# Attention scores and transposes in 64-row tiles of the TensorE array, values as plain fp32 products in two column halves

## The chip, the cores and the metric

The kernel runs on one core of a Trainium2 chip. The metric is the device time of one execution in microseconds (us), lower is better. The engines of the core work side by side: TensorE multiplies matrices (PE in the profile, with its weight loads as PEld), VectorE (DVE), ScalarE (ACT) and GpSimd (POOL) do the rest, and SyncE (SP) issues DMAs. A product of TensorE has a stationary operand, loaded into the array by a weight load, and a moving operand, which streams through column by column; the result lands in PSUM, in banks of 512 fp32 columns.

## The reference

Two layers of multi-head latent attention beside a convolution branch, followed by a gated feed-forward network, over 1024 tokens of width 1024, all in fp32. The change touches the attention alone:

```
q_nope, k_nope: 8 heads x 64      q_rope: 8 heads x 32      k_rope: 32, shared by the heads
sc = einsum("bqhd,bkhd->bhqk", qn, k_nope) + einsum("bqhr,bkr->bhqk", qr, k_rope)
p  = softmax(sc * scale)
o  = einsum("bhqk,bkhd->bqhd", p, v)          # v: 8 heads x 64
```

## The kernel before

Everything fp32 is multiplied as a pair: `hi` is the value rounded to fp32r, the type that TensorE takes at full rate, and `lo` the rest. A product is three products: hi·hi, hi·lo and lo·hi. Activations lie transposed, with channels on the partitions and the 1024 tokens along the row.

A layer has three stages: projections (`project`), attention (`attention`), and output projection with feed-forward network (`feed`). Instructions are emitted in the order of the Python code, and each engine runs its own in that order.

`attention` runs over 64 steps a layer: 8 heads times 8 blocks of 128 queries. In step n, TensorE is given three pieces of work:

- `values` (L1537): the product of exponentials and values. `v` holds for each key block and pair of heads 128 columns: 64 with the high part and 64 with the low part of the values of one head. The exponentials come as `pt`, transposed and split into hi and lo. A step does a quarter of 512 queries: 4 products of 128 rows by 512 columns (L1552) into the bank `o`. After four steps `o` holds the two partial sums in its two halves of the partitions, which ACT and DVE add (L1557, L1558).
- `turn` (L1514): transposes of the exponentials of a pair of query blocks, half of the keys at a time: 8 transposes of 128 by 128 (L1529) into two banks `t`. ACT rounds each bank to `pt` hi (L1531), DVE subtracts to `pt` lo (L1532).
- `scores` (L1492): the scores of the block two steps ahead. The stationary operand is `q` (96 rows: 64 of the head and 32 rotary), the moving one `k`; three products for each half of the keys make 6 of 512 columns (L1500). DVE then takes the maximum (L1502).

`expo` (L1505) is ACT's exponential of the block of the next step. PSUM holds two score tiles of two banks each and four single banks that `t`, `o` and small tiles share.

Beside this a table of 64 steps (`agenda`) places work of other kinds: taps of the long convolution that remain from the projections (`tap_late`, L1703), each of kind "pool" (GpSimd multiplies, a DMA adds), "act" (ScalarE multiplies in two halves, a DMA adds) or "both" (GpSimd multiplies and adds), the division by the sums, the splitting of finished heads, and the loads of the output weights `wo`. `LATE_KINDS` gives the kinds in turn, and `LATE_COST` how far apart they are placed.

Head 0 is put together by DMAs straight from the projections, the others are loaded from DRAM eight steps ahead (`load_head`, L1459).

## Time and profile before

| | us |
|---|---|
| median of 3 runs | 2284.3 (2283.11 to 2286.27) |
| span of the profiled execution | 2282.9 |
| attention of layer 0, about | 200 to 415 |
| attention of layer 1, about | 1330 to 1545 |

The profiled execution is one of the same program. Its span runs from the first to the last instruction; the median of the runs is 1.4 us above it. The granted TensorE clock is 0.999 of full over the span.

How to read it: a busy share says how long an engine had something in work, and an engine that is busy all the time is the bound wherever nothing releases it late. Durations of matmuls overlap, since one starts while the one before is still leaving the array; what a product costs in a row of products is the distance between starts, which the chain of waits gives, and not its own duration.

### The profile page before, as it was taken

How to read it: one execution, taken by the hardware profiler on the slowest of the kernel's cores; microseconds unless marked ns; L12 is line 12 of the kernel's file. 1: busy time of each engine (PE TensorE's matmuls, PEld its weight loads, DVE VectorE, ACT ScalarE, POOL GpSimd, SP SyncE). 2: the span in 40 equal slices, each digit the busy share in tenths (PEclk: the TensorE clock that was granted, in tenths of full speed). 3: DMA queues.
4: the chain of work that ended last, by engine and by line, in shares of the span. 5: the costliest groups of instructions: out<-in, count | busy, mean ns of one | idle time of the engine just before them, and what ended most of it. 6: DMA issues, size and time to landing. Idle time of an engine off the chain costs nothing.

```text
span 2282.9 us, 30530 instructions
## 1 busy us (share of the span) xinstructions
PE 2269.7 (99%) x10684; PEld 1887.8 (83%) x10684; DVE 1730.2 (76%) x2329; ACT 1286.7 (56%) x2043; POOL 781.8 (34%) x810
## 2 busy tenths in 40 slices
PE   9999999999999999999999999999999999999998
PEld 7888888888888888888888888888888888888887
DVE  6989888768877776776559788886697777768665
ACT  5445877646655555544533468774475555555444
POOL 1222787522333333001412237873323333320032
PEclk9999999999999999999999999999999999999999
DMA  6889998946899998935968999967659999989356
GB/s 185 165 175 271 194 200 166 235 138 145 211 277 296 275 296 208 334 106 143 209 136 166 218 255 197 184 149 207 175 129 228 271 302 279 294 210 315 102 124 167
DMA packets 198569, 475.73 MB, mean 208 GB/s; under 512 B 27296, under 2 KB 34576, under 8 KB 198416
## 3 DMA queue, kind: packets, MB, share of 16 engines
q0 software_dynamic: 103136, 222.46, 48.5%
q1 hardware_dynamic: 94992, 250.93, 32.9%
q8 instruction: 84, 1.38, 0.3%
q14 instruction: 69, 0.57, 0.1%
q10 hardware_dynamic: 288, 0.39, 0.0%
HBM read 309.28 MB, written 80.40 MB: 171 GB/s over the span
## 4 chain that ended last, share of the span: by engine, by line
PE 92%; DVE 3%; DMA 1%; POOL 1%; ACT 1%; issue 1%; SPq 0%; DVEq 0%; ACTq 0%; POOLq 0%
PE p L1063 36%; PE pd L1251 18%; PE s L1500 7%; PE po L874 7%; PE o L1552 4%; PE t L1529 4%; PE pa L215 2%; PE pg L215 2%; PE pg L513 2%; DVE conv L1694 2%; PE pq L215 1%; PE pn L215 1%; PE pv L1481 1%; PE pkv L215 1%; PE pa L513 1%
## 5 line engine op out<-in xcount | busy, mean ns | idle before, releaser
L1063 PE MATMUL p<-b,w 128*128 128x512 f32 x3552 | 806.3, 389 | 0.1
L1063 PEld LDWEIGHTS p<-b,w 128*128 128x128 f32 x3552 | 666.4, 188 | 139.3 <-DVE w L1441 0.5
L1251 PE MATMUL pd<-ab,wd 128*128 128x512 f32 (+1 forms) x1920 | 422.3, 381 | 0.0
L1251 PEld LDWEIGHTS pd<-ab,wd 128*128 128x128 f32 x1920 | 350.7, 188 | 69.5 <-DVE ab L1441 0.4
L1500 PE MATMUL s<-k,q 96*128 96x512 f32 x768 | 208.0, 406 | 0.0
L179 POOL DMA_DIRECT2D w<-wu x96 | 84.7, 883 | 360.0 <-ACT w L178 319.1
L1532 DVE TENSOR_TENSOR pt<-t,pt 128x512 fp32r<-128x512 f32 x256 | 164.8, 685 | 53.6 <-ACT pt L1531 51.7
L1711 POOL TENSOR_TENSOR late<-gate,par 128x1018 f32<-128x1018 f32 (+12 forms) x79 | 171.7, 2174 | 18.7 <-issue 9.7
L1531 ACT CAST pt<-t 128x512 fp32r<-128x512 f32 x256 | 137.6, 589 | 65.2 <-PE t L1529 63.6
L1453 DVE SCALAR_TENSOR_TENSOR o<-zg,par,o 128x1023 f32<-128x1023 f32 x88 | 112.7, 1283 | 75.6 <-ACT o L1447 74.3
L179 POOL DMA_DIRECT2D w<-in_w_up x116 | 100.5, 866 | 199.4 <-ACT w L178 175.4
L1502 DVE TENSOR_REDUCE mx<-s 128x1 f32<-128x1024 f32 x128 | 155.8, 1217 | 0.0
L1500 PEld LDWEIGHTS s<-k,q 96*128 96x128 f32 x768 | 135.1, 189 | 22.9 <-ACT p L1510 0.2
L1510 ACT ACTIVATE p<-s,mx 128x1024 f32<-128x1024 f32 x128 | 144.8, 1131 | 1.9 <-DVE mx L1502 1.9
L1694 DVE SCALAR_TENSOR_TENSOR conv<-gate,par,conv 128x1009 f32<-128x1009 f32 (+7 forms) x112 | 142.3, 1274 | 3.6 <-ACT conv L575 1.0
L1552 PE MATMUL o<-pt,v 128*128 128x512 f32 x512 | 140.3, 397 | 0.0
L837 POOL DMA_DIRECT2D wd<-in_w_down x44 | 32.6, 744 | 307.9 <-PE pd L1251 306.9
L1439 ACT CAST ab<-ac 128x512 fp32r<-128x512 f32 x130 | 80.1, 617 | 98.3 <-DVE ac L1186 95.6
L178 ACT ACTIVATE w<-w 128x512 fp32r<-128x512 f32 x212 | 133.6, 630 | 3.0
L1529 PEld LDWEIGHTS t<-ident,p 128*128 128x128 f32 x1024 | 119.6, 140 | 18.5 <-ACT p L1510 1.2
L1529 PE MATMUL t<-ident,p 128*128 128x128 f32 x1024 | 133.3, 273 | 0.7 <-ACT p L1510 0.7
L1012 DVE TENSOR_TENSOR zg<-p,zg 128x512 f32<-128x512 f32 x88 | 60.5, 690 | 96.5 <-PE p L1063 89.6
(2122 smaller groups left out, 4113.9 us busy)
## 6 DMA issues: line engine op xcount, KB each, us to landing
w<-in_w_up POOLq DMA_DIRECT2D x232, 256.0 KB, 7.2
wu<-in_w_up SPq DMA_DIRECT2D x88, 512.0 KB, 6.0
w<-wu POOLq DMA_DIRECT2D x96, 256.0 KB, 5.9
sd<-in_w_down SPq DMA_DIRECT2D x44, 512.0 KB, 10.1
ws<-sd SPq DMA_DIRECT2D x44, 512.0 KB, 7.4
wd<-in_w_down POOLq DMA_DIRECT2D x88, 256.0 KB, 5.3
act<-v SPq DMA_DIRECT2D x36, 512.0 KB, 5.7
ac<-act SPq DMA_DIRECT2D x72, 256.0 KB, 6.1
```

Source lines behind the costliest of these rows:

```text
L179: self.nc.gpsimd.dma_start(out=lo, in_=src, accum_op=ALU.add)
L215: nc.tensor.matmul(ps[:, HALVES[c]], w, x[:, HALVES[c]], start=(k == 0 and s == 0), stop=(k == n - 1 and s == 2))
L874: self.nc.tensor.matmul(ps, p[:, sl], q[:, cs], start=(k == 0 and t == 0), stop=(k == 3 and t == 2))
L1063: nc.tensor.matmul(ps, w[p][:, k * 128:(k + 1) * 128], b[:, q], start=(i in (1, 5, 2) and k == 0 and t == 0), stop=(k == 3 and t == 2), sk ...
L1251: nc.tensor.matmul(ps[t, m][:, cs], w[i, j][p][:, m * 128:(m + 1) * 128], b[:, q, cs], start=(i in (1, 5, 2) and j == 0 and s == 0), stop= ...
L1500: nc.tensor.matmul(ps[:, cs], q[i][0:96, qs], k[j][0:96, cs], start=(s == 0), stop=(s == 2))
L1502: nc.vector.tensor_reduce(out=mx, in_=ps, op=ALU.max, axis=AX.X, negate=True)
L1529: nc.tensor.transpose(tp[:, i, qi * 128:(qi + 1) * 128], st["p"][2 * qp + qi][:, kt * 128:(kt + 1) * 128], self.ident)
L1532: nc.vector.tensor_tensor(out=lo, in0=tp, in1=hi.bitcast(F32), op=ALU.subtract)
L1552: nc.tensor.matmul(po, v[2 * c + i][:, h // 2, e, :], pt[s][:, i, :], start=(c == 0 and i == 0 and s == 0), stop=(c == 3 and i == 1 and s ...
L1694: self.nc.vector.scalar_tensor_tensor(out=y[:, lo:hi], in0=u[:, lo + s:hi + s], scalar=self.tap(l, j, t), in1=y[:, lo:hi], op0=ALU.mult, o ...
L1711: self.nc.gpsimd.tensor_tensor(out=p[:, lo:hi], in0=u[:, lo + s:hi + s], in1=self.tap(l, j, t).broadcast_to([128, hi - lo]), op=ALU.mult)
```

## The change

- **Scores** (`scores`): the array is used as two tiles of 64 rows. Rows 0 to 63 compute the first half of the keys and rows 64 to 127 the second half, each into its own bank. The queries lie twice on the partitions (`qh`, `ql`: 64 rows of the head each; `qr`: 32 rotary rows high and 32 low), and the keys lie with their first half on the upper 64 partitions and the second on the lower (`kn`, and `keys` for the shared rotary part). Five passes of two products take the place of three passes of two.
- **Transposes** (`turn`): 16 transposes of 64 rows by 128 columns, in the same two row tiles, take the place of 8 of 128 by 128. The two tiles write two banks, `t0` and `t1`, of one buffer each. ACT copies `t0` and DVE copies `t1` into `pt`, unsplit, in fp32.
- **Values** (`values`): `v` and `pt` are plain fp32. The products run once for two turns: 8 products of 256 columns for a pair of query blocks. Each has 64 columns of values, and they go by turns to the left and the right column half of the array, with outputs in the two halves of the partitions of `o`. The sum of the halves (`gather`) is put behind the step's other work.
- **PSUM**: two score tiles as before, two shared banks where there were four, and `t0` and `t1`.
- **Heads**: loading a head takes 16 DMAs where it took 10, and the shared rotary keys are laid out once a layer by 8 DMAs.
- **Late taps**: one "act" in five of the first half becomes "pool"; GpSimd's multiplication is a tensor_scalar in place of a tensor_tensor with a broadcast operand; the costs that space the taps are smaller for "pool" and "both".

```diff
-LATE_KINDS = (("pool", "both", "act", "pool", "act"), ("pool", "both", "pool", "pool", "pool"))
-LATE_COST = {"act": 1.1, "pool": 3.5, "both": 4.8}
+LATE_KINDS = (("pool", "both", "act", "pool", "pool"), ("pool", "both", "pool", "pool", "pool"))
+LATE_COST = {"act": 1.1, "pool": 2.4, "both": 3.7}
+ROW_TILES = (slice(0, 64), slice(64, 128))
...
-        with self.psum(f"attn{l}", 2, 4):
+        with self.psum(f"attn{l}", 2, 2):
...
-            vt = self.blk(f"v{l}_{tt}", F32R, (128, 4, 2, 128))
...
+            if tt % 2 == 0:
+                v.append(self.blk(f"v{l}_{tt}", F32, (128, 2, 512)))
+            (nc.vector.tensor_copy if tt % 2 else nc.scalar.copy)(out=v[tt // 2][:, tt % 2], in_=ps)
...
-            for s, (i, j) in enumerate(((0, 0), (0, 1), (1, 0))):
-                for cs in HALVES:
-                    nc.tensor.matmul(ps[:, cs], q[i][0:96, qs], k[j][0:96, cs], start=(s == 0), stop=(s == 2))
+            passes = ((qh, kn, 0), (qh, kn, 1), (ql, kn, 0), (qr, keys, 0), (qr, keys, 1))
+            for s, (w, k, i) in enumerate(passes):
+                for r, cs in zip(ROW_TILES, HALVES):
+                    nc.tensor.matmul(ps[:, cs], w[r, qs], k[r, i, :], start=s == 0, stop=s == len(passes) - 1)
...
-                        nc.tensor.transpose(tp[:, i, qi * 128:(qi + 1) * 128], st["p"][2 * qp + qi][:, kt * 128:(kt + 1) * 128], self.ident)
-                hi, lo = (t[:, :, qs] for t in st["pt"][c, qp // 2])
-                nc.scalar.copy(out=hi, in_=tp)
-                nc.vector.tensor_tensor(out=lo, in0=tp, in1=hi.bitcast(F32), op=ALU.subtract)
+            tp = [self.pp.tile([128, 4, 2, 64], F32, name=f"t{l}_{h}_{qp}{g}{r}", tag=f"t{r}", bufs=1) for r in range(2)]
+            for i in range(4):
+                ks = slice((4 * g + i) * 128, (4 * g + i + 1) * 128)
                 for qi in range(2):
+                    for t, r in zip(tp, ROW_TILES):
+                        nc.tensor.transpose(t[:, i, qi, :], st["p"][2 * qp + qi][r, ks], self.ident[r, r])
+            pt = st["pt"][qp, g] = self.tmp("ws", f"pt{l}_{h}_{qp}{g}", F32, (128, 4, 2, 2, 64))
+            nc.scalar.copy(out=pt[:, :, :, 0, :], in_=tp[0])
+            nc.vector.tensor_copy(out=pt[:, :, :, 1, :], in_=tp[1])
...
-            for s in range(2):
-                for i in range(2):
-                    nc.tensor.matmul(po, v[2 * c + i][:, h // 2, e, :], pt[s][:, i, :],
-                                     start=(c == 0 and i == 0 and s == 0), stop=(c == 3 and i == 1 and s == 1))
+            for g in range(2):
+                pt = st["pt"].pop((qp, g)).rearrange("p k q r t -> p k (q r t)")
+                for i in range(4):
+                    k = 4 * g + i
+                    nc.tensor.matmul(po[ROW_TILES[i % 2], cs], v[k // 2][:, k % 2, h * 64:h * 64 + 64], pt[:, i, :],
+                                     start=k < 2, stop=k > 5)
...
+        for n in range(-2, total + 1):
+            if n % 2 and n > 2:
+                values((n - 3) // 2, n)
+            if n % 2 and n > 0 and n + 1 < total:
+                expo(n + 1)
+            if n > 0:
+                turn(n)
...
-            self.nc.gpsimd.tensor_tensor(out=p[:, lo:hi], in0=u[:, lo + s:hi + s],
-                                         in1=self.tap(l, j, t).broadcast_to([128, hi - lo]), op=ALU.mult)
+            self.nc.gpsimd.tensor_scalar(out=p[:, lo:hi], in0=u[:, lo + s:hi + s], scalar1=self.tap(l, j, t), scalar2=1.0,
+                                         op0=ALU.mult, op1=ALU.mult)
```

TensorE's rows in the middle of head 2 of layer 0, before: one step, with the scores of block 5, a quarter of the values of queries 0 to 511 and half of the transposes of blocks 2 and 3 (`s`, `o` and `t` are the PSUM tiles; `xN` joins equal neighbours).

```order
L1500 MATMUL s_2_5_2396<-k_20_1985,q_20_1983 128x512 x2
L1500 MATMUL s_2_5_2396<-k_21_1986,q_20_1983 128x512 x2
L1500 MATMUL s_2_5_2396<-k_20_1985,q_21_1984 128x512 x2
L1552 MATMUL o_2_0_2414<-pt_2_000_2307,v_0_1579 128x512
L1552 MATMUL o_2_0_2414<-pt_2_000_2307,v_1_1591 128x512
L1552 MATMUL o_2_0_2414<-pt_2_010_2308,v_0_1579 128x512
L1552 MATMUL o_2_0_2414<-pt_2_010_2308,v_1_1591 128x512
L1529 MATMUL t_2_12_2419<-ident,p_2_2_2334 128x128 x2
L1529 MATMUL t_2_12_2419<-ident,p_2_3_2372 128x128 x2
L1529 MATMUL t_2_13_2426<-ident,p_2_2_2334 128x128 x2
L1529 MATMUL t_2_13_2426<-ident,p_2_3_2372 128x128 x2
```

The same place on TensorE after the change: the scores of block 6, then all values of blocks 2 and 3, then the first four of 16 transposes of blocks 4 and 5.

```order
L1500 MATMUL s_2_6_2624<-kn_2_2057,qh_2_2054 128x512 x4
L1500 MATMUL s_2_6_2624<-kn_2_2057,ql_2_2055 128x512 x2
L1500 MATMUL s_2_6_2624<-kr_1132,qr_2_2056 128x512 x4
L1549 MATMUL o_2_0_2553<-pt_2_10_2582,v_0_1590 64x256 x2
L1549 MATMUL o_2_0_2553<-pt_2_10_2582,v_2_1607 64x256 x2
L1549 MATMUL o_2_0_2553<-pt_2_11_2621,v_4_1653 64x256 x2
L1549 MATMUL o_2_0_2553<-pt_2_11_2621,v_6_1705 64x256 x2
L1523 MATMUL t_2_200_2652<-ident,p_2_4_2562 128x64
L1523 MATMUL t_2_201_2653<-ident,p_2_4_2562 128x64
L1523 MATMUL t_2_200_2652<-ident,p_2_5_2637 128x64
L1523 MATMUL t_2_201_2653<-ident,p_2_5_2637 128x64
```

The values now stand in every second step alone, between scores and transposes; the step between has transposes and scores only.

VectorE at that place, before: two subtractions for each turn, and the maximum of a block of scores.

```order
L1532 TENSOR_TENSOR pt_2_010_2308<-t_2_10_2382,pt_2_000_2307 128x2x256
L1532 TENSOR_TENSOR pt_2_011_2310<-t_2_11_2389,pt_2_001_2309 128x2x256
L1502 TENSOR_REDUCE mx_2_5_2403<-s_2_5_2396 128x1
L1532 TENSOR_TENSOR pt_2_012_2346<-t_2_12_2419,pt_2_002_2345 128x2x256
L1532 TENSOR_TENSOR pt_2_013_2348<-t_2_13_2426,pt_2_003_2347 128x2x256
```

VectorE there after the change, with the sum of the halves of `o` (`yt`) between a maximum and the copy behind it, which happens in every second pair of steps.

```order
L1526 COPY pt_2_20_2670<-t_2_201_2653 128x8x64
L1502 TENSOR_REDUCE mx_2_7_2684<-s_2_7_2673 128x1
L1563 TENSOR_TENSOR yt_2_2551<-o_2_0_2553,yt_2_2551 64x512
L1526 COPY pt_2_21_2709<-t_2_211_2692 128x8x64
L1502 TENSOR_REDUCE mx_3_0_2724<-s_3_0_2713 128x1
```

Two subtractions became one copy, which no longer follows a copy of ScalarE; `pt_2_21` is what the second half of the next values reads.

More of the change, by code (lines that the diff above doesn't have):

```diff
@@ L525, in project @@
         kd = [self.dp.tile([HEADS, NOPE, T], F32R, name=f"kd{l}{i}") for i in range(2)]
-        krd = [self.dp.tile([ROPE, T], F32R, name=f"krd{l}{i}") for i in range(2)]
         st = {}
@@ L818, in project @@
         work(1e9)
-        return u, conv, away, (qd, qrd, kd, krd), (kvs, w["v"]), heads
+        return u, conv, away, (qd, qrd, kd), st["keys"], (kvs, w["v"]), heads
     def layer(self, l, carry):
@@ L1535, in turn, with values @@
                     st["p"].pop(2 * qp + qi)
-        def values(group, c, n):
-            h, gg = divmod(group, 2)
+        def values(pair, n):
+            h, qp = divmod(pair, 4)
             st = state[h]
             e = h % 2
+            gg = qp // 2
             main, aux = slice(e * 64, e * 64 + 64), slice(64 - e * 64, 128 - e * 64)
-            if c == 0:
+            if qp % 2 == 0:
                 if gg == 0 and e == 0:
```

93 lines of the change are left out of this document (36 added, 57 removed).

## The prediction

> **What bounds the kernel now.** I read the page from its top: the share of each engine, then the slices of TensorE, then the costliest groups.
>
> ```profile
> PE 2269.7 (99%) x10684; PEld 1887.8 (83%) x10684; DVE 1730.2 (76%) x2329; ACT 1286.7 (56%) x2043; POOL 781.8 (34%) x810
> PE   9999999999999999999999999999999999999998
> ...
> L1500 PE MATMUL s<-k,q 96*128 96x512 f32 x768 | 208.0, 406 | 0.0
> ...
> L1532 DVE TENSOR_TENSOR pt<-t,pt 128x512 fp32r<-128x512 f32 x256 | 164.8, 685 | 53.6 <-ACT pt L1531 51.7
> L1711 POOL TENSOR_TENSOR late<-gate,par 128x1018 f32<-128x1018 f32 (+12 forms) x79 | 171.7, 2174 | 18.7 <-issue 9.7
> L1531 ACT CAST pt<-t 128x512 fp32r<-128x512 f32 x256 | 137.6, 589 | 65.2 <-PE t L1529 63.6
> ...
> L1502 DVE TENSOR_REDUCE mx<-s 128x1 f32<-128x1024 f32 x128 | 155.8, 1217 | 0.0
> ...
> L1510 ACT ACTIVATE p<-s,mx 128x1024 f32<-128x1024 f32 x128 | 144.8, 1131 | 1.9 <-DVE mx L1502 1.9
> ...
> L1552 PE MATMUL o<-pt,v 128*128 128x512 f32 x512 | 140.3, 397 | 0.0
> ```
>
> TensorE is idle for 13 us in all (2282.9 less 2269.7). So the time changes by what TensorE's own work in the attention changes, and by waits that it does not have today. The stage itself, in the view of busy time by windows (the middle of the attention of layer 0; the columns are PE, PEld, DVE, ACT, POOL):
>
> ```profile
> 222.00:390.00 168.00, 168.00 (x953) 142.12 (x952) 140.90 (x177) 134.91 (x244) 136.54 (x89) 1.00 0.89 189
> ```
>
> Nothing but TensorE is full here, at full clock. What a step costs it stands in the chain of waits of that stretch, in order of time (start, length, what):
>
> ```profile
> 222.05 0.93 PE o L1552 x4
> 222.98 0.87 PE t L1529 x8
> 223.85 1.39 PE s L1500 x6
> 225.24 0.94 PE o L1552 x4
> 226.17 0.88 PE t L1529 x8
> 227.05 1.39 PE s L1500 x6
> ```
>
> A step is 3.20 us: values 0.93, transposes 0.87, scores 1.39. One product of 512 columns costs 0.232 (1.39 / 6), one transpose 0.109. Two steps, the unit of the changed kernel, are 6.40 us, and there are 32 such pairs in each of two layers, 64 in all.
>
> **The change, part by part.** I count one pair of steps.
>
> *Scores.* Six products become ten, in five pairs that use different rows of the array and different banks. No two products of the trace use different rows, so the price is bounded: from five times one product (pairs at once) to ten. I take pairs at once, because each product uses only half of the rows, and because the weight loads allow it:
>
> ```profile
> L1500 PEld LDWEIGHTS s<-k,q x768: 186/188/192, 203.2 to 1537.0; 96*128 96x128 f32 x192
> L1500 PE MATMUL s<-k,q x768: 387/393/479, 203.5 to 1537.2; 96*128 96x512 f32 x192
> L1569 PEld LDWEIGHTS sr<-ident,sums x14: 84/84/84, 250.4 to 1521.1; 128*8 128x8 f32 x14
> L1529 PEld LDWEIGHTS t<-ident,p x1024: 137/140/143, 213.0 to 1546.0; 128*128 128x128 f32 x171
> ```
>
> A load of 8 columns takes 84 ns, so some 80 are fixed, and one of 128 columns in the scores (188) occupies about 0.11. Even if ten loads follow each other, they take 1.1 us, beside 5 x 0.232 = 1.16. Two steps: 2.32 in place of 2.78.
>
> *Transposes.* Eight of 128 columns become 16 of 64 columns in row pairs. The moving part of one halves, to 0.055, but each still loads 128 columns of weights: 140 less 84 for 120 columns is 0.060 a load. Pairs that load at once give 8 x 0.060 = 0.48 a turn; loads that follow each other give 16 x 0.060 = 0.96, against 0.87 now. I take pairs at once, for the same reason as in the scores, plus 0.05 at the start of each scores burst, whose loads (0.11) are longer than a transpose that would cover them. Two turns: 1.06 in place of 1.75, with 2.02 as the other end. That choice carries most of the forecast. The Trainium skill speaks for it: TensorE: Matmul & The Clock Gate, Part 3, The mechanism, says that a weight load overlaps matmuls in flight when it goes to another row group. No run here shows it; by that rule the sum stays as it is, and without it the first rival below holds.
>
> *Values.* Eight plain fp32 products of 256 columns replace eight of 512. Plain products stand only at the very start, where eleven of them warm the array; the rows are of the view by line, and of TensorE's timeline:
>
> ```profile
> L397 PEld LDWEIGHTS warm<-ones x22: 289/333/333, 1.1 to 5.5; 128*128 128x128 f32 x22
> ...
> 1.06 5.06 PE L397 MATMUL warm<-ones 128*128 128x128 f32 x22 [1.06 <-DVE ones L372]
> 5.77 0.77 PE L468 MATMUL pg<-xs_0h,wg00h 128*128 128x512 f32 x1
> 7.30 0.50 PE L468 MATMUL pg<-xs_0h,wg00h 128*128 128x512 f32 x1 [0.76 <-ACT xs_0h L415]
> ```
>
> Eleven products are 22 records: a plain product is two loads and two passes. Less the last record's 421 ns, the starts of 22 passes of 128 columns lie over 4.64 us, 0.22 apart. But the load takes 333 ns there against 188 later, and the first full product 0.77 against 0.50, so the array ran at about half speed, whatever clock the profile gives for those microseconds. At full speed 128 columns are 0.11, and a pass of 256 columns 0.22 (the other end, if it was at full speed, is 0.44). Eight products are 16 passes. Each waits for the pass before it in its own column half, and the two passes of one product share a half, so a second pass runs beside the first pass of the next product: nine rounds of 0.22, 1.98 us, in place of 1.87. If the halves do not overlap it is 16 x 0.22 = 3.52; if the first and last pass overlap too, 1.76.
>
> *Changes of form.* In each pair of steps the array goes from row halves to column halves and back. A product's record is 393 ns, its share in a row of products 232: 0.16 us pass until its results are out. I take that once for each change, 0.32. The ends are nothing, and 0.16 plus a whole load, 0.35 each or 0.70. The Trainium skill, TensorEngine Tiling (Array Packing), Key Properties, says that a change of tiling mode drains the array; that speaks against this change, and by it the 0.32 is owed and not the zero. No row of this trace shows a drain.
>
> *Sum.* 2.32 + 1.06 + 1.98 + 0.32 = 5.68, against 6.40.
>
> *What waits instead.* ACT loses two copies of 0.59 in each step for one, DVE two subtractions of 0.69 for one copy that I price at 0.69 as well (a plain copy from PSUM by DVE is not in the trace; 0.59, as on ACT, to 0.69). Per pair DVE has two maxima (1.22), two copies and half a sum of halves (0.69): 4.2 us of 5.68. ACT has two exponentials with their read-out, two copies and half a copy of `o`:
>
> ```profile
> 337.80 0.21 ACT L1510 ACTIVATION_READ_ACCUMULATOR p<-s,mx 128x1 f32 x1
> ```
>
> that is 2 x (1.13 + 0.21 + 0.59) + 0.29 = 4.15. Both fit. But `t0` and `t1` have one buffer each: the second turn waits until both copies of the first are done, 0.16 + 0.69 after its transposes, while the scores between them run for 1.16. So 0.3 us of slack, which a late tap on ACT (0.73) or a cast of a finished head takes away now and then. The values read the second turn's `t1` copy, which stands behind a maximum and every second time behind the sum of halves: 0.2 (tail and signal) + 1.22 + 0.69 + 0.69 = 2.8 us after the scores of that maximum. By then TensorE has the second turn, the next scores and the first half of the values, which reads the first turn's copy: 0.53 + 1.16 + 1.0 = 2.7. That about covers. I add 0.10 a pair for these: **5.78 us, 0.62 less, 40 us in 64 pairs**; the ends of this item are 0 and 0.3.
>
> *The rest.* GpSimd has five more taps a layer; at the old 2.17 us plus 0.93 for their DMA issue that is 15 us of the 31 that it has free in the 168 us window, so costless as long as the stage shortens by less than the other 16. Its new multiplication is not in the trace; at the old price nothing is gained, and a cheaper one only adds slack. The view of waits has the place where it would show:
>
> ```profile
> PE po L874 <- DMA wo<-in_w_o: 1.9, 2, 1.0
> ```
>
> The output weights come by GpSimd's DMAs, behind its last additions, and TensorE already waits for them. With the six more DMAs for each head, which SP issues eight steps ahead, and the shorter cover at both ends I add 5 us (0 to 10). The row of copies for `v` shrinks, off the path.
>
> So 2282.9 - 40 + 5 = 2248, and the median of the runs lies 1.4 above that span: **2249 us**.
>
> **Rivals.**
> - *Weight loads follow each other* although the products do not (slower than before). Place: the 2048 small transposes. Then a turn is 0.96, the pair 6.74, 22 us more than now, with the 5 at the ends **2311**. It decides from 0.54 us more a pair, which is when a transpose costs over 0.047 on average. For it: no row shows two loads at once. Against: no load in the trace goes to other rows than the one before it, so none could show it.
> - *The gain is eaten*: the changes of form cost 0.70 and the copies 0.3 or a little more: 5.68 + 0.38 + 0.3 = 6.36 and the 5 us, **about 2287**, between 2268 and 2300. For it: single buffers, and slack of 0.3 us.
> - *Column halves follow each other*: 3.52 for the values, pair 7.32, **2348**. Against: different columns, different output partitions.
> - *The tiles do not work at once at all*, so the change does not do what it says: 4.64 + 2.02 + 3.52 + 0.42 = 10.6 a pair, **2558**.
> - *Plain passes cost 0.44*: nine rounds 3.96, **2376**.
> - *All hides*: no price for the form, eight rounds: 5.14 a pair and no waits, **about 2204**.
>
> **How the numbers follow.** The forecast (2232 to 2268) has 0.47, the eaten gain 0.17, loads in a row 0.15, all hidden 0.08, column halves in a row 0.07, no overlap 0.03, dear passes 0.03. A measurement tells a difference of about 0.2%, 4.6 us. Faster: 0.47 + 0.08 + 0.06 of the eaten gain = 0.61; within: 0.06; slower: the remaining 0.05 and the other four, 0.33. The range from 2222 to 2318 leaves out part of the hidden case, the column halves, no overlap and dear passes, about 0.2.
>
> **What would show it.** In the changed profile's chain, scores of ten products over 1.16 us a step and 16 transposes over half a microsecond show that rows work at once; 0.96 or more is the first rival, and starts of two loads of a pair 0.06 apart would name it. The values should be 16 records over 2 us, by twos. Gaps ahead of `o` and behind it, without a releaser, are the changes of form; waits of `t` for ACT or DVE the single buffers. TensorE should stay above 97% busy; if it falls, the second rival holds. I am wrong from the root if the ten products of a step take 2.3 us, or if the time of the attention, some 215 us a layer now, does not shrink by about 20.

## The result, and the profile after

| | before | after |
|---|---|---|
| median of the runs, us | 2283.8 (4 runs, 2283.11 to 2286.27) | 2319.6 (4 runs, 2314.6 to 2323.93) |
| ratio, 95% interval | 1 | 1.0154 (1.0136 to 1.0171) |
| span of the profiled execution, us | 2282.9 | 2312.6 |
| first scores to last values, two layers, us | 217.5 + 218.0 | 226.0 + 229.7 |

The change costs 36 us where 35 us of gain were forecast. The profiled execution is the fastest of the four (2314.6 us), so some 5 of the 36 us are not in the trace read here. The page of the changed kernel begins like that of before, and says little:

```profile
PE 2247.6 (97%) x12732; PEld 1798.7 (78%) x12732; DVE 1659.3 (72%) x2177; ACT 1215.3 (53%) x1873; POOL 736.1 (32%) x819
```

TensorE is busy for 22 us less and idles 65 us in place of 13. Now the chain of waits of the changed kernel in the middle of the attention (start, length, what):

```profile
243.97 0.64 PE t L1523 x16
244.61 1.22 PE s L1500 x10
245.83 0.58 PE t L1523 x16
246.41 1.22 PE s L1500 x10
247.62 1.88 PE o L1549 x16
249.50 0.64 PE t L1523 x16
```

Two turns, two scores and the values of a pair: 0.64 + 1.22 + 0.58 + 1.22 + 1.88 = 5.54 us, where the forecast's own work was 5.68 and the kernel before needs 6.40. TensorE does what was expected of it. Pairs that wait for no load start 5.44 to 6.04 us apart, about 5.7 in the mean. The time is lost elsewhere, and the busy time by windows says where. First the kernel before, over the attention of each layer (columns: length, then PE, PEld, DVE, ACT, POOL, granted clock, share of the 16 DMA engines, GB/s), and then the changed one:

```profile
203.50:421.00 217.50, 217.14 (x1217) 183.19 (x1216) 183.25 (x238) 171.65 (x313) 163.91 (x111) 1.00 0.90 205
1333.00:1551.00 218.00, 217.64 (x1219) 183.75 (x1218) 180.83 (x237) 170.71 (x312) 160.25 (x108) 1.00 0.88 200
```

```profile
207.00:433.00 226.00, 204.28 (x2240) 139.42 (x2239) 145.38 (x162) 136.34 (x230) 138.65 (x113) 0.95 0.97 222
1349.80:1579.50 229.70, 201.40 (x2241) 137.46 (x2240) 145.82 (x162) 136.17 (x230) 132.60 (x109) 0.93 0.93 213
...
222.00:390.00 168.00, 156.35 (x1820) 107.37 (x1820) 111.80 (x126) 109.11 (x187) 110.82 (x91) 0.97 1.02 219
```

Three columns matter. TensorE's busy time falls from 434.8 to 405.7, but the windows are 455.7 long: it now idles 50 us, from 0.7. The granted clock falls from 1.00 to 0.95 and 0.93. The stretches at half clock in the two windows last 54.6 us; TensorE is busy for 37.0 of them, and full clock would have saved half of that, some 18 us. And the DMA engines, at 0.89 of the same 168 us before, stand at 1.02. (The share adds up the times of all packets, packets overlap, and it is no hard limit: e6_taps_undone reaches 1.05. That the engines hold the loads up is for the experiments to show.) So the attention's bill is 48 us of work saved (434.8 - 405.7 + 18.5), 18 lost to the clock and 49 to waits, together 20 more; the other 9.5 us of the 29.7 between the spans lie outside these windows. What TensorE waits for, in the view of waits of the changed kernel (total, times, longest):

```profile
PE s L1500 <- DMA kn<-kd: 27.5, 7, 9.3
PE t L1523 <- ACT pt L1525: 11.3, 2, 7.9
PE s L1500 <- DMA ql<-qn: 4.8, 2, 4.1
PE o L1549 <- DVE yt L1563: 4.8, 8, 1.7
```

The first row is the keys of a head, loaded from DRAM, and the third the queries of head 0. The second is ScalarE's copy, held up behind its rounding of output weights that GpSimd's DMAs bring late (8.64 us before 1554.64). The DMA queues over the attention of layer 0, before and after (q0 is GpSimd's, with the additions of the late taps; q1 is SP's, with the loads):

```profile
q0 software_dynamic: 7488, 23.93, 57.3%
q1 hardware_dynamic: 6897, 20.53, 32.3%
```

```profile
q0 software_dynamic: 7474, 23.88, 54.5%
q1 hardware_dynamic: 9864, 25.88, 42.2%
```

GpSimd's queue takes the same 123 to 125 us of 16 engines (57.3% of 217.5, 54.5% of 226). SP's went from 70 to 95 us. Together 195 became 218 us of engine time, and TensorE's own work there, 204 less 11 for the clock, is 193. That makes the transfers the first suspect: the loads, which share the engines with the additions, are what comes late. The 218 are no fixed bill: from 222 to 390 us SP's packets took 160 ns each here (43.1% of 16 engines for 7248 packets), and 187 in e1_no_late_dma (51.1% for 7348), where the additions are left out. SP's queue shows the slow loads (start, length of the issue):

```profile
294.81 3.35 SPq L124 DMA_DIRECT2D qr<-qrd  x2
298.21 0.45 SPq L124 DMA_DIRECT2D kn<-kd  x1
298.70 0.60 SPq L124 DMA_DIRECT2D qh<-qd  x1
299.35 1.93 SPq L124 DMA_DIRECT2D qr<-qrd  x2
301.33 1.54 SPq L124 DMA_DIRECT2D kn<-kd  x1
```

Many issues of a load take 1 to 1.7 us here; in e1_no_late_dma, at a share of 0.54, most take 0.45 to 0.6. (The kernel before has slow ones too, 1.2 to 1.7 us from 282.77 to 287.38, at 0.89.) A load's sixteen last 19 us (from 316.11 to 335.27) of the 22 that a head has at 5.44 us a pair.

A wait costs more than its length. TensorE's timeline at one of them, and the granted clock around it:

```profile
310.58 0.71 PE L1500 MATMUL s<-kn,qh 64*128 64x512 f32 x3
315.31 0.79 PE L1500 MATMUL s<-kn,qh 64*128 64x512 f32 x1 [4.02 <-DMA kn<-kd]
315.31 1.21 PE L1500 MATMUL s<-kn,ql 64*128 64x512 f32 x2
315.90 1.47 PE L1500 MATMUL s<-kr,qr 64*128 64x512 f32 x4
317.31 2.58 PE L1549 MATMUL o<-pt,v 128*64 128x256 f32 x16
...
321.11 0.64 PE L1500 MATMUL s<-kr,qr 64*128 64x512 f32 x4
```

```profile
315.30:318.70 3.40, 3.39 (x15) 1.99 (x17) 1.23 (x1) 0.00 (x0) 2.81 (x4) 0.51 1.04 201
318.70:322.00 3.30, 3.30 (x52) 2.43 (x50) 0.90 (x2) 1.79 (x3) 3.00 (x4) 1.00 1.06 243
```

After an idle gap of 4.0 us TensorE runs at half clock for 3.4 us: four rotary products take 1.47 us in place of 0.64. Half of 3.4 us, 1.7, is lost on top of the 4.0.

### The profile page after: what moved, and what is told of

The parts are those of the page before. It is cut to its first block, busy times and chain, and to the rows that moved or that the text cites. A ratio compares the mean times of both kernels' runs of the same rounds, so it can differ in the third digit from the quotient of the medians.

```text
span 2312.6 us, 34368 instructions
## 1 busy us (share of the span) xinstructions
PE 2247.6 (97%) x12732; PEld 1798.7 (78%) x12732; DVE 1659.3 (72%) x2177; ACT 1215.3 (53%) x1873; POOL 736.1 (32%) x819
## 4 chain that ended last, share of the span: by engine, by line
PE 78%; DMA 10%; DVE 5%; POOL 2%; issue 2%; ACT 2%; SPq 1%; DVEq 0%; POOLq 0%; ACTq 0%
PE p L1066 33%; PE pd L1254 18%; PE po L877 6%; PE s L1500 3%; DMA kn<-kd 2%; PE pa L216 2%; PE o L1549 2%; PE pg L216 2%; DMA conv<-late 2%; PE pg L514 2%; DVE conv L1691 2%; PE pn L216 1%; PE pq L216 1%; DMA wo<-in_w_o 1%; PE t L1523 1%
## 5 line engine op out<-in xcount | busy, mean ns | idle before, releaser
L1526 DVE COPY pt<-t 128x512 f32<-128x512 f32 x128 | 87.9, 686 | 76.0 <-PE t L1523 74.7
L1549 PE MATMUL o<-pt,v 128*64 128x256 f32 x1024 | 133.8, 403 | 6.1 <-DVE yt L1563 4.8
L1708 POOL TENSOR_SCALAR late<-gate,par 128x1018 f32<-128x1018 f32 (+13 forms) x88 | 121.7, 1383 | 12.1 <-PE pn L216 6.3
L1500 PE MATMUL s<-kn,qh 64*128 64x512 f32 x512 | 97.9, 444 | 27.6 <-DMA kn<-kd 27.5
L1456 DVE SCALAR_TENSOR_TENSOR v<-zv,par,v 128x1023 f32<-128x1023 f32 x88 | 112.2, 1277 | 10.5 <-ACT v L1450 10.4
L1549 PEld LDWEIGHTS o<-pt,v 128*64 128x64 f32 x1024 | 70.9, 143 | 61.3 <-issue 26.1
L1442 ACT CAST w<-wu 128x512 fp32r<-128x512 f32 x84 | 51.8, 619 | 122.4 <-DVE wu L1015 122.4
L1523 PEld LDWEIGHTS t<-ident,p 64*128 64x128 f32 x2048 | 78.0, 139 | 49.0 <-issue 26.9
## 6 DMA issues: line engine op xcount, KB each, us to landing
sd<-in_w_down SPq DMA_DIRECT2D x44, 512.0 KB, 10.1
```

Source lines behind the costliest of these rows:

```text
L1456: self.nc.vector.scalar_tensor_tensor(out=o[:, a:b], in0=z[:, at + a:at + b], scalar=self.par[l][:, tap:tap + 1], in1=o[:, a:b], op0=ALU.m ...
L1500: nc.tensor.matmul(ps[:, cs], w[r, qs], k[r, i, :], start=s == 0, stop=s == len(passes) - 1)
L1549: nc.tensor.matmul(po[ROW_TILES[i % 2], cs], v[k // 2][:, k % 2, h * 64:h * 64 + 64], pt[:, i, :], start=k < 2, stop=k > 5)
```

## The experiments

Each ran beside the kernel before on the same chip; its median there is 2283.8 to 2284.7 us. "Pair" is the distance between the starts of two bursts of values.

**The additions of the late taps by DMA, left out** (the convolution's result lacks these taps).

```diff
         if kind == "both":
             ...
-        else:
-            self.nc.gpsimd.dma_start(out=y[:, lo:hi], in_=p[:, lo:hi], accum_op=ALU.add)
```

> The changed kernel without the DMAs that add the late taps of kinds pool and act to the convolution (39 a layer, so those taps are missing from the sum; everything else is the same). Theory DMA: the 16 DMA engines are full in the attention (busy share 0.97 in 203 to 425 us, where the kernel before had 0.89), and these additions are about half of their work, so the head loads land late. Then the waits of the scores for kn and ql (32 us) fall below 6 us, pairs of steps stand at 5.4 to 5.9 us throughout, and the time falls to 2225 to 2250 us. Theory SP: the 16 issues a head and the round trip of the sums in the SyncE queue set when the loads start, whatever the DMA engines do. Then at least half of the waits for kn stay (over 14 us), and the time stays above 2275.

2272.9 us, ratio 0.995 (0.9933 to 0.9967). The waits for keys, and the middle of the attention:

```profile
PE s L1500 <- DMA kn<-kd: 6.2, 4, 2.3
```

```profile
222.00:390.00 168.00, 163.14 (x1945) 111.97 (x1942) 120.00 (x135) 116.60 (x199) 73.31 (x55) 0.98 0.54 111
```

Without them the DMA share falls to 0.54, the loads come nearly in time and 47 us are back: the transfers' part is shown. But the kernel stays above the 2225 to 2250 expected; two slow pairs at the start and two at the end of each layer (10.3 and 7.5, 12.8 and 10.0 us in layer 0; 10.1 and 7.2, 6.8 and 8.3 in layer 1) are still there. So transfers in the middle were not all.

**Half of each load issued by ScalarE**, the second row tile's eight DMAs.

```diff
-                self.move(tiles[p][r, :], qd[p][h])
+                queue = self.nc.scalar if c else None
+                self.move(tiles[p][r, :], qd[p][h], queue)
...
```

> The changed kernel with half of each head's loads (the 8 DMAs of the lower 64 partitions) issued by ScalarE in place of SyncE. The bytes are the same. Theory SP: with 8 issues a head SyncE is done in time, the waits for kn fall from 27 to below 8 us, and the time falls to 2270 to 2290. Theory DMA: the loads share the same full engines, the waits of TensorE for loads stay above 20 us in sum (for whichever tile is last), and the time stays at 2305 to 2340, more if ScalarE is held up by its own issues.

2390.1 us, ratio 1.0464 (1.0449 to 1.048). The waits for keys are gone, and TensorE waits 99.8 us for exponentials instead, 14 times up to 14.3: ScalarE's exponentials stand behind its own issues and what those wait for (63.0 us for key loads alone). Issuing from a second engine only stopped that engine. Since TensorE now comes later to every load, the run decides nothing for SP's queue itself.

**Half of the late additions by GpSimd instead of DMA.**

```diff
-LATE_KINDS = (("pool", "both", "act", "pool", "pool"), ("pool", "both", "pool", "pool", "pool"))
+LATE_KINDS = (("both", "pool", "act", "both", "pool"), ("both", "pool", "both", "pool", "both"))
```

> The changed kernel with about 15 late taps a layer moved from kind pool (a DMA adds) to kind both (GpSimd adds). All taps are computed. About 15 x 3 us of DMA work a layer is gone, 216 to about 171 us, and GpSimd has some 22 us more. Theory DMA: most of the waits for kn go (below 10 us), the time falls to 2235 to 2275. Theory SP: the time stays within 10 us of the changed kernel's 2320, since SyncE's issues are untouched.

2287.9 us, ratio 1.0016 (1.0003 to 1.0028), with the whole computation done: 32 us of the loss are back, less than the DMA theory's 2235 to 2275, far more than the 10 us of the other. What is left of the waits for keys (18.3 us in 4) is all at the load of head 1, which stands on SP's queue behind the spills (the stores to DRAM) of the queries.

**The row tiles one after the other**: in scores and transposes all instructions of one tile, then all of the other; in the values two products of one column half, then two of the other.

```diff
-            for s, (w, k, i) in enumerate(passes):
-                for r, cs in zip(ROW_TILES, HALVES):
+            for r, cs in zip(ROW_TILES, HALVES):
+                for s, (w, k, i) in enumerate(passes):
...
```

> The changed kernel with the same products and transposes in another order: in each group all of one tile first, then all of the other (scores 5 + 5, transposes 8 + 8, values column half 0 twice, then half 1 twice). If it is the alternation that lets two tiles work at once, scores go from 1.22 to about 2.1 us a step, transposes from 0.62 to about 0.9 to 1.0, values from 1.9 to about 3.1 a pair, and the whole to 2450 to 2520 us. If the price is set by something else (loads, or the products' own rate), the durations stay within 10% of the changed kernel.

One time, 2316.0 us: as the changed kernel, where 2450 to 2520 were expected if alternation mattered. The chain of waits (pieces of one or two instructions between these are left out):

```profile
244.00 0.76 PE t L1523 x13
...
244.94 1.08 PE s L1500 x8
...
246.15 0.47 PE t L1523 x10
...
246.80 1.38 PE s L1500 x9
248.19 1.93 PE o L1549 x16
```

A pair takes 6.1 us, 0.65 more than in turns, and not the double: transposes and scores alternate in the chain in pieces smaller than a turn, so one tile's work can still run beside the other's, and the values cost 1.93 with their halves by twos. And 0.65 us x 62 pairs, 40 us more work, cost nothing in this one run: the waits for keys fell from 27.5 to 11.8 us. That fits a stage that is bound by something else.

**A head's load in 8 DMAs in place of 16**, same bytes.

```diff
...
-                for i in range(2):
-                    at = c * 64 + p * ROPE + i * HALF
-                    self.move(tiles[2][at:at + HALF, :], qrd[p][i, h])
-                self.move(tiles[3][r, p, :], kd[p][h][:, HALVES[c]])
+            self.move(tiles[2][r, :], qrd[:, :, h])
+            self.move(tiles[3][r, :, :], kd[:, h, :, HALVES[c]].rearrange("p d t -> d p t"))
```

> The changed kernel, with a head's load in 8 DMAs in place of 16: the rotated query rows of both halves and both key parts come in one DMA each per row tile (the spills lie in one buffer for it). The bytes and the packets stay as they are. Theory A (the number of issues on SP's queue is what makes the loads late: 16 issues of 1 us and more, and the wait for the sums' way through memory, are more than the 21.8 us of a head): TensorE's waits for the key tile fall from 27.5 us to under 8, and the time to 2280 to 2297. Theory B (the transfer engines are full, and an issue only takes long because it waits for room): the issues take twice as long each, the waits for the key tile stay at 18 to 30 us, the time at 2310 to 2326.

2379.7 us, ratio 1.042 (1.0404 to 1.0436). Neither theory: a key DMA now lands after 18.4 us (median; 7.8 in the changed kernel), and from the middle of a load on, of SP's packets in the trace only about 4 and then 1 to 2 are under way at a time. The run e8_before_more_traffic suggests why.

**The taps' table of before** in the changed kernel.

```diff
-LATE_KINDS = (("pool", "both", "act", "pool", "pool"), ...
-LATE_COST = {"act": 1.1, "pool": 2.4, "both": 3.7}
+LATE_KINDS = (("pool", "both", "act", "pool", "act"), ...
+LATE_COST = {"act": 1.1, "pool": 3.5, "both": 4.8}
```

> The changed kernel with the late taps' table of before (which of them ScalarE computes, and the costs that spread them over the steps); the cheaper form of POOL's product stays. Theory of full transfer engines: each late tap of either kind ends in the same addition by DMA, so that the traffic stays, and the time stays within 0.3% of the changed kernel's (2313 to 2326), with the waits for the key tile at 20 to 30 us. Rival (the table itself costs the time: POOL has more to do and its DMAs are issued in bunches): the waits for the key tile fall under 12 us and the time to 2285 to 2300.

2314.4 us, ratio 1.0128 (1.0102 to 1.0154), waits for keys 39.1 us: the table is not the cause.

**Merged loads, thinned additions, everything earlier.** The edits of e5_merged_loads and e3_more_both, each head's load two steps earlier, the second head's ahead of the last four spills, the output weights asked for at step 53 and completed one step later.

```diff
-                if qt == 2 and h + 1 < HEADS and h + 1 not in loaded:
+                if qt == 0 and h + 1 < HEADS and h + 1 not in loaded:
...
+            if j == 1:
+                heads[1] = self.load_head(l, 1, qd, qrd, kd)
...
```

> The changed kernel with everything that the traces name as late put right: half of the late additions by POOL instead of DMA, 8 DMAs a head, each head's load issued two steps earlier and the second head's ahead of the last four spills, the output projection's weights asked for two steps earlier and completed one step later. If late transfers (and the half clock behind each gap) are all that keeps the changed kernel from its 5.44 to 5.98 us per pair of steps, the long pair at the start (16 us) and those at the end (11 us) go too: 2235 to 2260. If POOL or ScalarE is next in line, pairs of 6.5 us and more stay all through the attention: 2270 to 2290.

2317.2 us, ratio 1.0143 (1.0128 to 1.0158): a miss, with 43.2 us of waits for keys. They come with the merged DMAs: e9_all_early_16_loads, the same kernel with 16 loads, has 7.9.

**The kernel before with more traffic**: six copies of 43 rows behind each load.

```diff
...
+        for i in range(6):
+            self.move(self.more[i], qd[i % 2][h][0:43, 0:512])
```

> The kernel before with six more DMAs per head behind each load (43 rows of 2048 bytes each, memory to memory, into a buffer that nothing reads): about the extra packets that the changed kernel moves. Theory (the traffic only hurts because a pair of steps became shorter: 6.40 us a pair, 25.6 us a head, still leaves room): within 0.5% of before, 2283 to 2295, DMA share 0.93 to 0.99 in the middle of the attention, TensorE's waits for the key and query tiles under 6 us. Rival (the transfer engines have no room left at all in the kernel before): waits of 15 us and more, 2300 to 2325.

2557.1 us, ratio 1.1198 (1.1179 to 1.1217), far beyond both expectations, with the DMA engines nearly idle:

```profile
274.34 23.14 SPq L123 DMA_DIRECT2D more<-qd  x8
```

```profile
277.00:286.00 9.00, 8.75 (x35) 7.38 (x36) 4.53 (x5) 3.89 (x7) 0.62 (x2) 0.68 0.07 27
```

A share of 0.07 is one engine of 16. A DMA of 43 rows went through a single engine; eight such issues took 23 us, and what stood behind them on the queue waited. The Trainium skill, DMA: Bandwidth & Descriptors, Why a DMA increments its semaphore by 16 and not by 1, states the rule: a DMA uses the largest number of engines up to 16 that divides the slowest dimension of both its sides. 43 is prime, which leaves one, and the trace agrees with its 0.07. The merged rotary load of e5_merged_loads has outer dimensions of 2 by 2 in DRAM and falls under the same rule, which fits its few packets at a time; so that run was no test of the number of issues.

**Everything early, with the 16 loads.** The kernel of e7_all_loads_early with the loads of the changed one.

> The run with all loads early again, but with a head's load in its 16 DMAs as in the changed kernel: half of the late additions by POOL, each head's load issued two steps earlier, the second head's ahead of the last four spills, the output projection's weights asked for two steps earlier and completed one step later. In the runs with merged DMAs the loads ended on 4 and then on 1 transfer engine at a time, which held them up whatever their number. Theory (late transfers, and the half clock behind each gap, are all that keeps the changed kernel from its 5.44 to 5.98 us a pair): the long pair at the start of each layer's attention (16 to 17 us) falls under 9, the three at the end (30 us together) under 24, 2250 to 2270. Rival (the gaps only move to another place): 2283 to 2292 as with the POOL additions alone.

2277.4 us, ratio 0.9966 (0.9949 to 0.9983): a little faster than before, but not the 2250 to 2270 expected. Waits for keys 7.9 us; nearly all pairs take 5.44 to 6.01. The start of layer 0 is clean, layer 1 still has a pair of 10.6 us there, and two pairs of 10.0 to 10.1 us stand at the end of each layer.

**The kernel before with even traffic**: four copies of 64 rows behind each load.

```diff
...
+        for i in range(4):
+            self.move(self.more[i], qd[i % 2][h][:, HALVES[i // 2]])
```

> The kernel before with four more DMAs per head behind each load (64 rows of 2048 bytes each, memory to memory, into a buffer that nothing reads), spread evenly over the transfer engines, where the earlier 43 rows went through one engine after another. Theory (a pair of steps of 6.40 us, 25.6 us a head, still leaves room for this traffic): 2283 to 2297, TensorE's waits for the key and query tiles under 8 us in all. Rival (no room in the kernel before either: the extra traffic alone costs what the changed kernel lost): waits of 15 us and more, 2300 to 2325.

2287.6 us, ratio 1.0016 (1.0006 to 1.0026), no wait for keys or queries among its longest. The middle of the attention:

```profile
222.00:390.00 168.00, 166.77 (x943) 140.74 (x942) 139.45 (x176) 134.19 (x243) 136.47 (x89) 1.00 0.93 209
```

The share rises to 0.93, and the pair of 6.4 us still has room. The four DMAs carry 512 KB a head, as much as the changed kernel's loads carry more than those before (though into DRAM, not SBUF). Such traffic alone costs 3 us; to do the harm seen, it needs the shorter pair.

**Key rows whole**: `kd` laid out so that a head's keys of one half come as 64 rows of 4096 bytes.

```diff
...
-                self.move(tiles[3][r, p, :], kd[p][h][:, HALVES[c]])
+            self.move(tiles[3][r, :, :].rearrange("d p t -> d (p t)"), kd[h, :, c].rearrange("d p t -> d (p t)"))
```

> The run e9_all_early_16_loads, with the keys spilled so that a head's high and low part of one half lie side by side in memory: the key tile then comes in 2 DMAs of 64 rows of 4096 bytes in place of 4 of 2048 (14 issues a head, half as many key packets, the same bytes). Theory of full transfer engines (a packet of 2048 bytes took 98 ns alone and one of 4096 bytes 173): it saves 256 x (2 x 98 - 173) / 2 ns, some 3 us over 16 engines per head at most 0.2, so nothing: within 0.3% of e9_all_early_16_loads. Rival (the number of issues on SP's queue counts): 0.3 to 0.8% faster than it.

2276.2 us, ratio 0.9962 (0.9949 to 0.9975): the same as e9_all_early_16_loads. Two issues fewer in each load do not show (its key spills take twice as many as there).

**GpSimd done earlier**: e11_key_rows_whole with the late taps over 51 steps and the convolutions' sums from step 55.

```diff
-SIDE_TIME = 56
-TOTAL_TIME = 60
+SIDE_TIME = 51
+TOTAL_TIME = 55
```

> The run e11_key_rows_whole with GpSimd's late taps spread over 51 steps in place of 56, and its three sums of the convolutions from step 55 in place of 60. In the runs with hardly a load wait left the last two pairs of each layer still take 10 us each: VectorE's product of the last heads took 4.69 us there (0.65 before), while GpSimd added the convolutions. Theory (the two engines hold each other up there, and TensorE drops to half clock in the gap): the last two pairs fall to 6 to 8 us, 2262 to 2271. Rival (the end waits for other things, or the taps now crowd the loads): 2274 to 2295.

2273.4 us, ratio 0.9949 (0.9932 to 0.9965), not to be told from the 2276.2 without it, where 2262 to 2271 were expected. The end of layer 0 (VectorE, then GpSimd):

```profile
398.04 0.65 DVE L1584 SCALAR_TENSOR_TENSOR yt<-yt,rb 64x512 f32<-64x512 f32 x1
...
401.69 3.04 DVE L1584 SCALAR_TENSOR_TENSOR yt<-yt,rb 64x512 f32<-64x512 f32 x1
```

```profile
401.53 2.65 POOL L200 TENSOR_TENSOR ys_5l<-yt,ys_5h 128x1024 fp32r<-128x1024 f32 x1
```

The same product of VectorE takes 0.65 us, and 3.04 where it meets an elementwise operation of GpSimd that began 0.16 us before: it ends 0.55 us after that one does. The Trainium skill, SBUF — State Buffer, SBUF: two separate sides, has this as an exclusive lock: of an operation of VectorE with two SBUF inputs and one of GpSimd that reads SBUF, the one that starts second waits until the first has ended, and the rows agree. Moving the sums of the convolutions only put another operation (`ys_5l`) in their place, and the last two pairs still take 8.8 and 10.6 us in layer 0, 7.5 and 9.6 in layer 1.

**The taps' part of the change alone**, in the kernel before (its table, costs and the cheaper product).

> The kernel before with the change's taps alone: GpSimd's cheaper product, its table of late taps and its costs. Nothing waits for GpSimd in the kernel before, and the additions by DMA stay as many: 2280 to 2290. Rival (the table crowds the transfers by itself): 2295 and more, with TensorE waiting for the query or key tiles.

2283.9 us, ratio 0.9998 (0.9988 to 1.0007): nothing, as expected. The cheaper product is real (1383 ns by the changed kernel's row, 2174 before); nothing waits for it.

**The scores of before in the changed kernel**: 96 rows, six products, 10 DMAs a head.

```diff
-            passes = ((qh, kn, 0), (qh, kn, 1), (ql, kn, 0), (qr, keys, 0), (qr, keys, 1))
-            for s, (w, k, i) in enumerate(passes):
-                for r, cs in zip(ROW_TILES, HALVES):
-                    nc.tensor.matmul(ps[:, cs], w[r, qs], k[r, i, :], start=s == 0, stop=s == len(passes) - 1)
+            for s, (i, j) in enumerate(((0, 0), (0, 1), (1, 0))):
+                for cs in HALVES:
+                    nc.tensor.matmul(ps[:, cs], q[i][0:96, qs], k[j][0:96, cs], start=(s == 0), stop=(s == 2))
...
```

> The changed kernel with the scores of before (96 rows, three products, 10 DMAs a head), and the values, transposes and copies of the change. Two scores cost 0.46 us more a pair by their rows (1.39 against 1.16 each): 5.9 to 6.0 us a pair. Theory (it is the larger loads of the new scores that the transfers have no room for): the waits for key and query tiles under 8 us and 2265 to 2285. Rival (any pair that is shorter than 6.40 us starves the loads, since the taps' additions fill the transfers in the time of the attention): waits of 15 us and more, 2290 to 2312.

2286.9 us, ratio 1.0013 (1.0003 to 1.0022): 3 us above before and slightly above the 2265 to 2285 expected, with no wait for keys or queries and TensorE busy throughout at full clock:

```profile
222.00:390.00 168.00, 168.00 (x1591) 114.27 (x1590) 111.95 (x126) 107.38 (x182) 118.35 (x100) 1.00 0.90 189
```

But its pair is 6.32 to 6.45 us, where 5.9 to 6.0 were expected. TensorE's timeline:

```profile
301.42 1.95 PE L1545 MATMUL o<-pt,v 128*64 128x256 f32 x16
303.29 0.71 PE L1519 MATMUL t<-ident,p 64*128 64x64 f32 x16
303.93 1.66 PE L1496 MATMUL s<-k,q 96*128 96x512 f32 x6
305.52 0.71 PE L1519 MATMUL t<-ident,p 64*128 64x64 f32 x16
306.16 1.19 PE L1496 MATMUL s<-k,q 96*128 96x512 f32 x4
```

From start to start: values 1.87, turn 0.64, scores 1.59 (1.39 before). Two of the latter and the values make 6.33. So the new transposes and values by themselves gain 0.07 us a pair: what they save, the old scores beside them lose. Practically the whole gain of the change on TensorE hangs on the new scores (6.33 to 5.44), and the whole extra traffic too. So no run has the shorter pair without the larger loads, and how much each of the two does to the waits stays open.

**The same with all that was put earlier** in e9_all_early_16_loads (the same edits).

> The run e15_old_scores with what e9_all_early_16_loads has (half of the late additions by GpSimd, loads and output weights earlier). By the pairs alone it is 62 x 0.2 us = 12 us behind e9_all_early_16_loads, by its smaller loads ahead. Theory (with the additions thinned, the transfers no longer decide, and the shorter pair does): 2280 to 2290, behind it. Rival (the transfers still decide there): 2262 to 2275, ahead.

2298.8 us, ratio 1.0063 (1.0047 to 1.008): both theories missed. The pairs are again 6.32 to 6.45 and no load is late, but the fall of the DMA share from 0.90 to 0.67 buys nothing, and the first values come 3.6 us later and the last two pairs of layer 0 take 9.1 and 10.6 us in place of 6.8 and 8.1. So thinning and moving cost some 12 us of their own here, and the other kernels that have them probably carry such a cost too.

**The first eight taps of each layer added by GpSimd**, on the kernel of e12_pool_done_earlier.

```diff
-        kinds = [LATE_KINDS[2 * i // len(late)][i % 5] for i in range(len(late))]
+        kinds = ["both" if i < 8 else LATE_KINDS[2 * i // len(late)][i % 5] for i in range(len(late))]
```

> The run e12_pool_done_earlier with the first eight late taps of each layer added by GpSimd itself, so that few additions by DMA run while the spills and the loads of heads 1 and 2 are on their way. Its one remaining load wait per layer (5.4 and 4.9 us, and 7 us more in two pairs at half clock) falls under 2 us: 2255 to 2266. Rival (GpSimd falls behind, and its later additions crowd the next loads or the end): 2270 to 2285.

2268.8 us, ratio 0.9928 (0.9914 to 0.9941), the best of all, 16 us under the kernel before and 3 above the 2255 to 2266 expected. No wait for keys or queries is left among its longest. Its attention:

```profile
206.30:415.60 209.30, 196.95 (x2241) 134.92 (x2240) 146.66 (x163) 133.79 (x226) 169.85 (x117) 0.98 0.86 190
1332.60:1533.60 201.00, 195.12 (x2241) 134.00 (x2240) 144.11 (x162) 133.51 (x226) 163.50 (x112) 0.99 0.86 192
```

TensorE idles 18 us here, from 50. Of these 5.3 are one wait where ScalarE's cast of a finished head stood behind GpSimd, now the fullest helper, with the transposes waiting for ScalarE; the others are mostly the two ends.

## Why the prediction was wrong, step by step

- **The price on TensorE: right.** Scores 1.22 a step (forecast 1.16), transposes 0.58 to 0.69 (0.53), values 1.88 to 2.04 (1.98). Pairs of different rows do run at once, and column halves overlap: the sum, 5.68 with 0.32 for changes of form, measured 5.54. No gap stands where the form changes; the other pieces are 0.18 dearer than forecast, and whether that is the change of form is not shown. By busy time the attention's own work fell by 48 us, against 46 forecast (0.72 x 64). What the forecast had not seen is that the parts depend on each other: with 96-row scores in between, the scores cost 1.59 and the new transposes and values gain 0.07 a pair.
- **Waits on copies (0.10 a pair): right in the middle of the attention.** Pairs there take 5.44 to 6.04 us, 5.7 in the mean, forecast 5.78. The waits for a copy that cost much (11.3 us in two) are at the ends, where ScalarE waits for output weights; the forecast had them in its next term, the cover at both ends.
- **"With the six more DMAs for each head, which SP issues eight steps ahead ... I add 5 us (0 to 10)": this is the step that failed.** It took "ahead" for "hidden". In the attention the waits cost 49 us (32 of them for keys and queries, 11 by the output weights, the rest mostly copies) and the half clock behind them 18, and 9.5 more lie outside: 77 us, where this term and the 0.10 a pair for copies held 11. One column of the forecast's own window row warned of it: a DMA share of 0.89 is 150 us of transfers in 168, and the stage was to shrink by a tenth while its loads grew. It said "Nothing but TensorE is full here" beside that row, and it counted issues where it had to count engine time. The runs: without the additions the key waits fall to 6.2 us and 47 us come back (e1_no_late_dma); with half of them 32 us come back (e3_more_both); 40 us more TensorE work cost nothing (e4_tiles_in_turn, one run); as much extra traffic beside the slower pair costs 3 us (e10_before_even_traffic); and with fewer additions and earlier loads 51 us come back with the whole computation done (e17_first_taps_no_dma).
- **What the transfers do not explain.** From the forecast of 2249, e1_no_late_dma is still 24 us away and e17_first_taps_no_dma 20. Some 9 of these lie outside the attention, the rest mostly at its two ends.
- **The clock was taken as given.** The forecast read 1.00 and kept it. A gap of 4 us costs 1.7 more in half clock; over both layers that is 18 us that no term held.
- **Outside the attention, 9.5 us.** Every kernel with the new scores has a wait of 3.1 to 3.3 us for `kvs_1h` in the projections, the two with the old scores 0.5 or less, and with the old scores the rest of the kernel is 2.4 us above before (span 2284.4 less windows of 434.6) instead of 9.5. Without the additions it is still 8.5 (e1_no_late_dma). So it comes with the new layout of keys and queries and not with the traffic in the attention; 2.5 of the 9.5 are idle time and 3.4 half clock (11.4 to 14.8 and 1308.5 to 1311.9 us). Which DMA or copy does it was not tried.
- **The rivals.** "The gain is eaten" had the sign of the outcome, but with the wrong eater (copies and forms, on TensorE's side), and 2319.6 lies above its 2268 to 2300. "Weight loads follow each other", 2311, came nearest by luck: its turn of 0.96 us measured 0.58 to 0.69. None was about transfers, though the kernel moves more bytes in less time.
- **The signs.** The time of the attention, which was to shrink by about 20 us a layer, grew by 8.5 and 11.7, so the forecast's own sign of being wrong came. The other, TensorE above 97% busy, did not tell: it is 97%, since 65 us of idle time are only 2.8% of the span and a TensorE at half clock counts as busy.

What stays open: the last two pairs of each layer, 9 to 10 us each in the best run (6.8 and 8.1 with the old scores in e15_old_scores). The lock between VectorE and GpSimd is seen there, but the run meant to clear it did not.

## What to carry to other kernels

Where a change shortens a stage, divide the stage's transfers by its new length, not by the old one; a helper at 0.89 leaves room for a gain of about a tenth, and traffic added in the same change comes on top. "Issued early" hides a latency, but not a queue that is full. And price each idle gap of TensorE of some 4 us at four tenths more, since it comes back at half clock.

## What the runs showed of the hardware

- A DMA of 43 rows ran on one of 16 engines (share 0.07), and copies of six such pieces per head cost 273 us; four of 64 rows cost 3.
- After an idle gap of 4.0 us TensorE ran at half clock for 3.4 us.
- At a DMA share of 1.02 many issues of a load on SP's queue took 1 to 1.7 us, at 0.54 most took 0.45 to 0.6. Issued by ScalarE, the loads held up its exponentials, and TensorE waited for them up to 14.3 us.
- Row tiles overlap in turns, and largely also with their instructions one after the other: a pair took 5.44 us and 6.1. Values with the column halves in turns took 1.88 to 2.04 us, by twos 1.93.
- Scores of 96 rows cost 1.39 us among transposes of 128 rows, and 1.59 among transposes in 64-row tiles.
- A product of VectorE from two SBUF operands took 0.65 us alone and 3.04 beside an elementwise operation of GpSimd.
